# RWKV-7 stage of a hybrid encoder layer on one Trainium2 core: the 16x16 substitution emitted behind the first products of the next unit, without ties to other operations

## Chip, cores and metric

The kernel runs on one core of a Trainium2 chip. Its time is the device time of one execution in microseconds (us), the median of the runs. Five engines work side by side, each through a list of instructions of its own, in order: TensorE (PE in the rows, its weight loads PEld), VectorE (DVE), ScalarE (ACT), GpSimd (POOL) and SyncE (SP), which here only issues DMAs.

## What is computed

One layer of an encoder over a sequence of 1024 positions with 1024 features: a combined projection, four sequence mixers (RWKV-7, mLSTM, RG-LRU, HGRN2), a gated sum of the four, and a convolutional feed-forward block. The change lies in the RWKV-7 mixer alone. Cut to its core:

```python
def _rwkv7_scan(r, logw, a, b, k, v):
    # S_t = S_{t-1} diag(w_t) + (S_{t-1} a_t) b_t^T + v_t k_t^T ;  y_t = S_t r_t
    def step(state, inp):
        r_t, lw_t, a_t, b_t, k_t, v_t = inp
        sa = jnp.einsum("bhvk,bhk->bhv", state, a_t)
        state = (state * jnp.exp(lw_t)[:, :, None, :]
                 + sa[..., None] * b_t[:, :, None, :]
                 + v_t[..., None] * k_t[:, :, None, :])
        return state, jnp.einsum("bhvk,bhk->bhv", state, r_t)
    ...
for d in range(2):      # forward and backward over the sequence, 8 heads of 64
    ...
    yd = _rwkv7_scan(*args)
```

The kernel doesn't step through the positions. It takes chunks of 64 and writes the dependence of the positions of a chunk on one another as a triangular system, whose inverse it builds: blocks of 16 by substitution, then blocks of 32 and 64 from these by products. The state passes from chunk to chunk.

## The kernel before

**Units.** `rwkv` works through 16 units, one for each pair of heads (4) and each stretch of 256 positions (4), both directions at once. A unit goes through these functions:

- `rw_lin` and `rw_dir`: decays and gates. `rw_dir` runs once for each direction: a load of its input (`rw_in`, L862, issued by SP), a scan on VectorE (L868), exponentials on ScalarE (L870, L872), GpSimd's L865 before them, then products on VectorE (L882, L884, L888, L890), with copies and products on GpSimd.
- `rw_first`: TensorE's products for the system (L920), masked by VectorE (L928) into `cb`; then the first half of `rw_solve`.
- `rw_solve`: SP sends `cb` out to DRAM (L985) and loads it back in another layout into `SB` (L989) and `pr` (L990). Here the function yields. Its second half is the **substitution**: a copy on ScalarE (L992) of `pr` into `SB`, then on VectorE a copy (L1000) and three rounds (n = 2, 4, 8) of products (L1010) and reduces (L1013), at the end of which `ST` holds the inverse blocks. SP sends `ST` out to DRAM (L1016, two DMAs, tile dT) and loads it back as `R` (L1019).
- `rw_second`: VectorE transposes `R` (L1035); TensorE multiplies (L1040, L1047, L1060, L1068) with VectorE's work between; the result `TF` is written by VectorE (L1071) and ScalarE (L1074).
- `rw_btm`: further products (L968) for the chain.
- `rw_chain`: the chain over the unit's four chunks. For each chunk: TensorE's L1125, ScalarE's copy s (L1128), TensorE's L1135, ScalarE's copy uv (L1138), TensorE's L1143 and L1151, and ScalarE's copy of the state (L1154, into M at the unit's end). The outputs y (L1106, L1110) are copied by ScalarE (L1113).

**The loop.** Step g of the loop runs three units side by side: the chain of the unit before (`prev`), `rw_second` of the current one (`cur`) and `rw_first` of the next (`fst`, `nxt`). It does so in four stages, st = 0 to 3, advancing the generators a piece at a time. Between these, `pieces()` lays 512-column products of the gate projection on TensorE, so that it has something to do while the other engines work; their weights are split into w_hi and w_lo by ScalarE (L116) and GpSimd (L119).

**What sets the order.** TensorE's order in this loop is the order of the code (`manual_schedule`). On the other engines a scheduler decides, from the order in which instructions are emitted, a raised priority for the chain's operations, and ties: inside `issue_after(x)`, instructions are placed behind the instruction x. The second half of `rw_solve`, substitution and DMAs, is emitted by the last `next(fst, None)` at st = 3, inside two such ties: to `self.act_mo`, the chain's last state copy (L1154), and to `self.dve_tf`, the last of the four TF copies on VectorE (L1071):

```python
if st == 3:
    if g + 2 < n:
        lin = self.rw_lin(*order[g + 2], wp)
    with ExitStack() as q:
        if prev is not None:
            q.enter_context(self.tc.issue_after(self.act_mo.ins))
        if cur is not None:
            q.enter_context(self.tc.issue_after(self.dve_tf.ins))
        next(fst, None)
```

Units are numbered here from 0, by the step in which `rw_second` is run on them; "unit 3" in the rows is the turn of the loop in which the L1040 of unit 3 follows the substitution of unit 3.

Of the kernel before, what the change touches and what calls it, by code (L numbers as in the profile page):

```python
# [23 lines left out]
class K:  # L24
# [996 lines left out]
    def rw_second(self, b, wp):  # L1021

        nc = self.nc
        NB = self.NB
        NC = 2 * NB
        cb = b["cb"]

        fl = lambda x: x.rearrange("p d m t -> p (d m t)")
        rs = lambda q: slice(32 * q, 32 * q + 32)

        blk = lambda q, d, m, sb: cb[rs(q), d, m, 32 * sb:32 * sb + 32]
        R = b["R"]
        RT = self.t(wp, [P, 2, NC, 32], "rw_RT")
        E = self.t(wp, [P, 2, NC, 32], "rw_E")
        nc.vector.transpose(fl(RT), fl(R))  # L1035
        dm = [(d, m) for d in range(2) for m in range(NC)]
        pe = self.ps([P, 2, NC, 32], "ps")
        for d, m in dm:
            for q in range(4):
                nc.tensor.matmul(pe[rs(q), d, m, :], lhsT=blk(q, d, m, q % 2), rhs=(RT, R)[d][rs(q), d, m, :],  # L1040
                                 start=True, stop=True, tile_position=(32 * q, 32 * q))
        nc.vector.tensor_tensor(E, pe, self.rw_lm.unsqueeze(2).to_broadcast([P, 2, NC, 32]), op=MUL)
        yield
        pe = self.ps([P, 2, NC, 32], "ps")
        for d, m in dm:
            for q in range(4):
                nc.tensor.matmul(pe[rs(q), d, m, :], lhsT=E[rs(q), d, m, :], rhs=(R, RT)[d][rs(q), d, m, :],  # L1047
                                 start=True, stop=True, tile_position=(32 * q, 32 * q))
        TT, Tn = R, RT
        for d in range(2):  # L1050
            nc.vector.tensor_tensor(TT[:, d], (R, RT)[d][:, d], pe[:, d], op=ADD)
        nc.vector.transpose(fl(Tn), fl(TT))
        yield

        TF = b["TF"] = self.rw_TFt[b["i"] % 2]
        qq = [(d, 2 * hf + d, 2 * hf + 1 - d) for d in range(2) for hf in range(2)]
        pe = self.ps([P, NC, 32], "ps")
        for m in range(NC):
            for d, q0, q1 in qq:
                nc.tensor.matmul(pe[rs(q1), m, :], lhsT=blk(q0, d, m, q1 % 2), rhs=Tn[rs(q0), d, m, :],  # L1060
                                 start=True, stop=True, tile_position=(32 * q0, 32 * q1))
        E3 = self.t(wp, [P, NC, 32], "rw_E")
        nc.vector.tensor_copy(out=E3, in_=pe)
        yield
        pe = self.ps([P, NC, 32], "ps")
        for m in range(NC):
            for d, q0, q1 in qq:
                nc.tensor.matmul(pe[rs(q0), m, :], lhsT=E3[rs(q1), m, :], rhs=TT[rs(q1), d, m, :],  # L1068
                                 start=True, stop=True, tile_position=(32 * q1, 32 * q0))
        for d, q0, q1 in qq:  # L1070
            self.dve_tf = nc.vector.tensor_copy(out=TF[rs(q0), d, :, 32 * (q1 % 2):32 * (q1 % 2) + 32], in_=pe[rs(q0)])  # L1071
        with self.tc.issue_after(self.act_uv.ins) if self.act_uv is not None else ExitStack():
            for q in range(4):
                nc.scalar.copy(TF[rs(q), :, :, 32 * (q % 2):32 * (q % 2) + 32], TT[rs(q)])  # L1074
        yield

    def rw_chain(self, b, wp):


        nc = self.nc  # L1080
        NB, j = self.NB, b["j"]
        M = self.rw_M
# [3 lines left out]
        NC = 2 * NB  # L1086
# [4 lines left out]
        def both(x, st, h, rows):  # L1091

            v = x[rows, 0, st, h, :]
            w = x[rows, 1, NC - 1 - st, h, :]
            return bass.AP(v.tensor, v.offset, [list(v.ap[0]), [w.offset - v.offset, 2], [1, 64]])
# [22 lines left out]
        for st in range(NC):  # L1118
            cs = (st, NC - 1 - st)
            with prio():  # L1120

                pt = self.ps([P, 2, 64], "pc")
                for d, c in enumerate(cs):
                    for h, hr, _ in halves:
                        nc.tensor.matmul(pt[hr, d, :], lhsT=b["ar"][d][:, c, 0, h, :], rhs=b["mv"][:, d, c, h, :],  # L1125
                                         start=True, stop=True, tile_position=(0, 64 * h))
                s = self.t(wp, [P, 2, 64], "rw_s")
                nc.scalar.copy(s, pt)  # L1128
            yield
            with prio():  # L1130

                pu = self.ps([P, 2, 64], "pc")
                for d, c in enumerate(cs):
                    for h, hr, _ in halves:
                        nc.tensor.matmul(pu[hr, d, :], lhsT=b["TF"][hr, d, c, :], rhs=s[hr, d, :], start=True, stop=True,  # L1135
                                         tile_position=(64 * h, 64 * h))
                for h, hr, _ in halves:
                    self.act_uv = nc.scalar.copy(both(b["uv"], st, h, hr), pu[hr])  # L1138

                pm = self.ps([P, 2, 64], "pc")  # L1140
                for d, c in enumerate(cs):
                    for h, hr, _ in halves:
                        nc.tensor.matmul(pm[hr, d, :], lhsT=b["dg"][hr, d, c, :], rhs=b["mv"][hr, d, c, h, :],  # L1143
                                         start=(d == 0), stop=True, tile_position=(64 * h, 64 * h), skip_group_check=True)
            if st:
                y(st - 1)
            yield
            with prio():
                for d, c in enumerate(cs):
                    for h, hr, _ in halves:  # L1150
                        nc.tensor.matmul(pm[hr, d, :], lhsT=b["btm"][:, d, c, hr], rhs=b["uv"][:, d, c, h, :], start=False,  # L1151
                                         stop=True, tile_position=(0, 64 * h), skip_group_check=True)
                for h, hr, _ in halves:
                    self.act_mo = nc.scalar.copy(M[j][hr, :, h, :] if st == NC - 1 else both(b["mv"], st + 1, h, hr), pm[hr])  # L1154
            if st == NC - 1:
                y(st)
            yield
        for d in range(2):
            n0 = b["n0"][d]
            for h, hr, _ in halves:  # L1160
# [3 lines left out]
                                    in_=src)  # L1164
# [109 lines left out]
    def rwkv(self, dr, dG, es, extra):  # L1274
        nc = self.nc
# [34 lines left out]
        cur = next(gen)  # L1310
# [2 lines left out]
        lin = self.rw_lin(*order[1], wp)  # L1313
        for j in range(self.VA, 4):
            self.rw_v(j, vp)
        prev = None

        with self.tc.manual_schedule(engines={mybir.EngineType.PE}):
            for g in range(n + 1):
                chn = self.rw_chain(prev, wp) if prev is not None else iter(())  # L1320
                sec = self.rw_second(cur, wp) if cur is not None else iter(())
                fst, nxt = iter(()), None
                for st in range(4):

                    next(chn, None)
                    if st > 1:
                        next(sec, None)
                    pieces(1)

                    next(chn, None)  # L1330
                    if st == 0:
                        if cur is not None:
                            self.rw_btm(cur, wp)
                        if g + 1 < n:
                            fst = self.rw_first(*order[g + 1], lin, wp)
                            nxt = next(fst)
                    else:
                        next(fst, None)

                    next(chn, None)  # L1340
                    if st > 1:
                        next(sec, None)
                    if prev is None:
                        pieces(self.GATE0 // 4 - 1)
                    else:
                        credit += rate if g < n else rate + self.ENDF / 2
                        k = int(credit + 1e-6)
                        credit -= k
                        pieces(k)
                    if st == 3:  # L1350
                        if g + 2 < n:
                            lin = self.rw_lin(*order[g + 2], wp)
                        with ExitStack() as q:
                            if prev is not None:
                                q.enter_context(self.tc.issue_after(self.act_mo.ins))
                            if cur is not None:
                                q.enter_context(self.tc.issue_after(self.dve_tf.ins))
                            next(fst, None)
                next(chn, None)
                prev, cur = cur, nxt  # L1360
            for _ in self.filler:
                pass
# [760 lines left out]
```

## Time and profile before

| | us |
|---|---|
| runs | 2766.28, 2766.10, 2759.79 |
| median | 2766.1 |
| profiled execution | 2765.5 |
| its span | 2763.7 |
| TensorE busy (PE) | 2529.6 (92%) |
| its weight loads (PEld) | 2026.5 (73%) |
| VectorE busy (DVE) | 1755.2 (64%) |
| GpSimd busy (POOL) | 1216.7 (44%) |
| ScalarE busy (ACT) | 953.2 (34%) |

The profile is of one execution. The span runs from its first instruction to its last; 1.8 us of the execution lie outside. The shares are means over the whole layer; the loop that the change touches runs from about 420 us to about 1060 us of the span, and what holds it up is to be read there. Idle time counts only on an engine that the end of the span hangs on. Of TensorE's clock the trace says what level was granted, 1.00 for 2.4 GHz and 0.50 for 1.2 GHz; the mean over the span is 0.961.

### The profile page before, as it was taken

How to read it: one execution, taken by the hardware profiler on the slowest of the kernel's cores; microseconds unless marked ns; L12 is line 12 of the kernel's file. 1: busy time of each engine (PE TensorE's matmuls, PEld its weight loads, DVE VectorE, ACT ScalarE, POOL GpSimd, SP SyncE). 2: the span in 40 equal slices, each digit the busy share in tenths (PEclk: the TensorE clock that was granted, in tenths of full speed). 3: DMA queues.
4: the chain of work that ended last, by engine and by line, in shares of the span. 5: the costliest groups of instructions: out<-in, count | busy, mean ns of one | idle time of the engine just before them, and what ended most of it. 6: DMA issues, size and time to landing. Idle time of an engine off the chain costs nothing. (4 is left out here: it accounts for less than half of the span.)

```text
span 2763.7 us, 48164 instructions
## 1 busy us (share of the span) xinstructions
PE 2529.6 (92%) x19138; PEld 2026.5 (73%) x19138; DVE 1755.2 (64%) x2741; ACT 953.2 (34%) x1781; POOL 1216.7 (44%) x1196
## 2 busy tenths in 40 slices
PE   5999888898898899889989989999998999999998
PEld 4777666676676677668777777788776788888887
DVE  6667765665664650665553668357479998896344
ACT  4355533343343342433331332211234344442002
POOL 3654463343443431742222355357555444445332
PEclk9999999999999999999999989999999999999999
DMA  6422243343443433421111444555543222225222
GB/s 211 132 69 65 92 138 91 104 105 97 105 113 83 103 76 113 112 60 43 39 43 29 123 156 153 179 186 164 168 122 96 84 76 88 73 73 196 87 80 77
DMA packets 402395, 290.46 MB, mean 105 GB/s; under 512 B 121339, under 2 KB 364521, under 8 KB 402169
## 3 DMA queue, kind: packets, MB, share of 16 engines
q1 hardware_dynamic: 380600, 252.18, 31.7%
q10 hardware_dynamic: 21568, 35.20, 3.6%
q8 instruction: 150, 2.46, 0.4%
q14 instruction: 77, 0.62, 0.1%
HBM read 223.47 MB, written 63.83 MB: 104 GB/s over the span
## 5 line engine op out<-in xcount | busy, mean ns | idle before, releaser
L119 POOL TENSOR_TENSOR w_lo<-w_raw,w_hi 128x512 fp32r<-128x512 f32 x284 | 393.2, 1385 | 798.3 <-ACT w_hi L116 272.7
L125 PE MATMUL pbig<-uh,w_hi 128*128 128x512 f32 x1208 | 509.7, 423 | 17.7 <-ACT w_hi L116 8.5
L127 PE MATMUL pbig<-uh,w_lo 128*128 128x512 f32 x1208 | 486.2, 404 | 6.1 <-POOL w_lo L119 5.8
L126 PE MATMUL pbig<-ul,w_hi 128*128 128x512 f32 x1184 | 478.3, 404 | 0.0
L125 PEld LDWEIGHTS pbig<-uh,w_hi 128*128 128x128 f32 x1208 | 234.5, 195 | 85.4 <-ACT gt L1239 11.4
L127 PEld LDWEIGHTS pbig<-uh,w_lo 128*128 128x128 f32 x1208 | 234.7, 195 | 62.5 <-POOL w_lo L119 10.2
L126 PEld LDWEIGHTS pbig<-ul,w_hi 128*128 128x128 f32 x1184 | 230.6, 195 | 42.7 <-issue 1.6
L118 DVE CAST w_hi<-w_raw 128x512 fp32r<-128x512 f32 x224 | 136.2, 610 | 174.1 <-PE pbig L126 120.5
L127 PE MATMUL ppc<-uh,w_lo 128*128 128x512 f32 x340 | 133.4, 396 | 1.4 <-POOL w_lo L119 1.0
L125 PE MATMUL ppc<-uh,w_hi 128*128 128x512 f32 x340 | 132.6, 394 | 1.2 <-DVE w_hi L118 1.2
L126 PE MATMUL ppc<-ul,w_hi 128*128 128x512 f32 x320 | 125.4, 392 | 0.0
L125 PE MATMUL ppa<-uh,w_hi 128*128 128x512 f32 x220 | 89.1, 405 | 5.6 <-DVE w_hi L118 5.6
L127 PE MATMUL ppa<-uh,w_lo 128*128 128x512 f32 x220 | 86.9, 395 | 0.8 <-POOL w_lo L119 0.8
L1138 ACT COPY rw_uv<-ppc 64x128 f32<-64x128 f32 x128 | 33.0, 258 | 158.1 <-PE ppc L1135 156.5
L127 PE MATMUL ppy<-uh,w_lo 128*128 128x512 f32 x216 | 85.0, 394 | 1.4 <-POOL w_lo L119 1.0
L1848 ACT CAST w_hi<-s 128x512 fp32r<-128x512 f32 x84 | 52.0, 619 | 97.5 <-PE ppc L126 19.8
L125 PE MATMUL ppy<-uh,w_hi 128*128 128x512 f32 x216 | 85.0, 393 | 0.1
L126 PE MATMUL ppa<-ul,w_hi 128*128 128x512 f32 x208 | 83.5, 402 | 0.0
L126 PE MATMUL ppy<-ul,w_hi 128*128 128x512 f32 x208 | 82.1, 395 | 0.0
L127 PEld LDWEIGHTS ppc<-uh,w_lo 128*128 128x128 f32 x340 | 64.1, 189 | 16.5 <-POOL w_lo L119 1.4
L125 PEld LDWEIGHTS ppc<-uh,w_hi 128*128 128x128 f32 x340 | 64.3, 189 | 15.7 <-DVE w_hi L118 2.1
L204 ACT CAST uh<-h_raw 128x1024 fp32r<-128x1024 f32 x22 | 23.0, 1051 | 148.6 <-PE ppc L127 121.2
(795 smaller groups left out, 6438.8 us busy)
## 6 DMA issues: line engine op xcount, KB each, us to landing
w_raw<-in_w_in_dram SPq DMA_DIRECT2D x172, 256.0 KB
ada_w<-in_ada_w_dram SPq DMA_DIRECT2D x24, 1024.0 KB
s_raw<-in_ffn_up_dram SPq DMA_DIRECT2D x84, 256.0 KB
dG<-gt ACTq DMA_DIRECT2D x64, 256.0 KB
sgt<-dG SPq DMA_DIRECT2D x32, 512.0 KB
rw_in<-dIn SPq DMA_DIRECT2D x32, 384.0 KB
w_raw<-in_ffn_down_dram SPq DMA_DIRECT2D x44, 256.0 KB
dF<-cv SPq DMA_DIRECT2D x22, 512.0 KB
```

Source lines behind the costliest of these rows:

```text
L118: nc.vector.tensor_copy(out=hi, in_=raw[:, k0:k0 + m])
L119: nc.gpsimd.tensor_tensor(lo, raw[:, k0:k0 + m], hi.bitcast(F32), op=SUB)
L125: nc.tensor.matmul(pt, lhsT=wh, rhs=uh, start=start, stop=False)
L126: nc.tensor.matmul(pt, lhsT=wh, rhs=ul, start=False, stop=False)
L127: nc.tensor.matmul(pt, lhsT=wl, rhs=uh, start=False, stop=stop)
L204: nc.scalar.copy(hi, src)
L1138: self.act_uv = nc.scalar.copy(both(b["uv"], st, h, hr), pu[hr])
L1848: nc.scalar.copy(hi, x)
```

## The change

The substitution and its DMAs are no longer emitted at the end of step g but in step g + 1, behind the first piece of the chain there (at st = 0: the first L1125 products and the copy s), and outside any tie. `pend` carries the generator over. The attributes `dve_tf` and `act_mo` go, since nothing reads them any more. No instruction is added or taken out.

```diff
--- before.py
+++ after.py
@@ -1068,7 +1068,7 @@
                 nc.tensor.matmul(pe[rs(q0), m, :], lhsT=E3[rs(q1), m, :], rhs=TT[rs(q1), d, m, :],
                                  start=True, stop=True, tile_position=(32 * q1, 32 * q0))
         for d, q0, q1 in qq:
-            self.dve_tf = nc.vector.tensor_copy(out=TF[rs(q0), d, :, 32 * (q1 % 2):32 * (q1 % 2) + 32], in_=pe[rs(q0)])
+            nc.vector.tensor_copy(out=TF[rs(q0), d, :, 32 * (q1 % 2):32 * (q1 % 2) + 32], in_=pe[rs(q0)])
         with self.tc.issue_after(self.act_uv.ins) if self.act_uv is not None else ExitStack():
             for q in range(4):
                 nc.scalar.copy(TF[rs(q), :, :, 32 * (q % 2):32 * (q % 2) + 32], TT[rs(q)])
@@ -1151,7 +1151,7 @@
                         nc.tensor.matmul(pm[hr, d, :], lhsT=b["btm"][:, d, c, hr], rhs=b["uv"][:, d, c, h, :], start=False,
                                          stop=True, tile_position=(0, 64 * h), skip_group_check=True)
                 for h, hr, _ in halves:
-                    self.act_mo = nc.scalar.copy(M[j][hr, :, h, :] if st == NC - 1 else both(b["mv"], st + 1, h, hr), pm[hr])
+                    nc.scalar.copy(M[j][hr, :, h, :] if st == NC - 1 else both(b["mv"], st + 1, h, hr), pm[hr])
             if st == NC - 1:
                 y(st)
             yield
@@ -1313,7 +1313,7 @@
         lin = self.rw_lin(*order[1], wp)
         for j in range(self.VA, 4):
             self.rw_v(j, vp)
-        prev = None
+        prev, pend = None, iter(())
 
         with self.tc.manual_schedule(engines={mybir.EngineType.PE}):
             for g in range(n + 1):
@@ -1323,6 +1323,8 @@
                 for st in range(4):
 
                     next(chn, None)
+                    if st == 0:
+                        next(pend, None)
                     if st > 1:
                         next(sec, None)
                     pieces(1)
@@ -1350,12 +1352,7 @@
                     if st == 3:
                         if g + 2 < n:
                             lin = self.rw_lin(*order[g + 2], wp)
-                        with ExitStack() as q:
-                            if prev is not None:
-                                q.enter_context(self.tc.issue_after(self.act_mo.ins))
-                            if cur is not None:
-                                q.enter_context(self.tc.issue_after(self.dve_tf.ins))
-                            next(fst, None)
+                        pend = fst
                 next(chn, None)
                 prev, cur = cur, nxt
             for _ in self.filler:
```

On TensorE all stands as before. On three other engines the order is another. The names end in numbers of the program's buffers, which can differ between the two kernels where the same tile is meant.

**ScalarE, at the start of the substitution of unit 3.** Before:

```order
L1138 COPY rw_uv_3406<-ppc_4331 64x2x64 x2
L1074 COPY rw_TF_190_720<-rw_R_3921 32x8x32 x4
L939 COPY rw_tmp_4355<-ppa_4352 2x256
L939 COPY rw_tmp_4358<-ppa_4352 2x256
L1154 COPY rw_M_719_3927<-ppc_4338 64x2x64 x2
L992 COPY rw_SB_4241<-rw_pr_4242 32x256
L1113 COPY rw_ysb_3929<-ppy_4343 128x2x2x64
```

After:

```order
L1138 COPY rw_uv_3406<-ppc_4331 64x2x64 x2
L1074 COPY rw_TF_190_720<-rw_R_3939 32x8x32 x4
L992 COPY rw_SB_4241<-rw_pr_4242 32x256
L939 COPY rw_tmp_4355<-ppa_4352 2x256
L939 COPY rw_tmp_4358<-ppa_4352 2x256
L1154 COPY rw_M_717_3896<-ppc_4338 64x2x64 x2
L1113 COPY rw_ysb_3898<-ppy_4343 128x2x2x64
```

The substitution's first copy, L992, stood behind L939 and the chain's L1154 and stands right behind the TF copies L1074. On VectorE the first ten instructions after it (L1000, four L1010, an L1013, four L1010) move likewise from behind the four L1071 to ahead of them.

**VectorE, in the middle of the substitution of unit 3**, where `rw_dir` of the unit after the next lies between its rounds. Before:

```order
L1013 TENSOR_REDUCE rw_ST_713<-rw_pr_4242 64x2x4x4
L1010 TENSOR_TENSOR rw_pr_4242<-rw_SB_4241,rw_ST_713 64x256
L1013 TENSOR_REDUCE rw_G_4443<-rw_pr_4242 64x32
L868 SCALAR_TENSOR_TENSOR rw_tmp_4549<-rwrs_717,rw_l_788_4429 128x256
L888 SCALAR_TENSOR_TENSOR rw_tmp_4562<-rw_l_789_4431,rw_in_4546 128x256
L1010 TENSOR_TENSOR rw_pr_4242<-rw_SB_4241,rw_ST_713 64x256
L868 SCALAR_TENSOR_TENSOR rw_tmp_4574<-rwrs_717,rw_l_791_4438 128x256
```

After:

```order
L1013 TENSOR_REDUCE rw_ST_713<-rw_pr_4242 64x2x4x4
L1010 TENSOR_TENSOR rw_pr_4242<-rw_SB_4241,rw_ST_713 64x256
L1013 TENSOR_REDUCE rw_G_4461<-rw_pr_4242 64x32
L1010 TENSOR_TENSOR rw_pr_4242<-rw_SB_4241,rw_ST_713 64x256
L1013 TENSOR_REDUCE rw_G_4461<-rw_pr_4242 64x32
L1010 TENSOR_TENSOR rw_pr_4242<-rw_ST_713,rw_G_4461 64x256
L868 SCALAR_TENSOR_TENSOR rw_tmp_4549<-rwrs_717,rw_l_788_4429 128x256
L888 SCALAR_TENSOR_TENSOR rw_tmp_4562<-rw_l_789_4431,rw_in_4546 128x256
L1013 TENSOR_REDUCE rw_ST_713<-rw_pr_4242 64x4x8
```

The first scan of `rw_dir` (L868) stood behind the first reduce into G of the last round (n = 8) and now stands behind that round up to its first L1010 of `ST` and G.

**VectorE, at the end of the substitution of unit 3.** Before:

```order
L890 SCALAR_TENSOR_TENSOR rw_BK_4554<-rw_tmp_4562,rw_tmp_4549 64x4x64 x2
L1013 TENSOR_REDUCE rw_ST_713<-rw_pr_4242 64x4x8
L888 SCALAR_TENSOR_TENSOR rw_tmp_4587<-rw_l_792_4440,rw_in_4571 128x256
L1010 TENSOR_TENSOR rw_pr_4242<-rw_ST_713,rw_G_4443 64x256
L890 SCALAR_TENSOR_TENSOR rw_BK_4579<-rw_tmp_4587,rw_tmp_4574 64x4x64 x2
L1013 TENSOR_REDUCE rw_ST_713<-rw_pr_4242 64x4x8
L1035 STREAM_TRANSPOSE rw_RT_4699<-rw_R_4471 128x256
```

After:

```order
L884 TENSOR_TENSOR rw_AR_4578<-rw_in_4571,rw_l_791_4438 64x4x64
L1013 TENSOR_REDUCE rw_ST_713<-rw_pr_4242 64x4x8
L890 SCALAR_TENSOR_TENSOR rw_BK_4554<-rw_tmp_4562,rw_tmp_4549 64x4x64 x2
L888 SCALAR_TENSOR_TENSOR rw_tmp_4587<-rw_l_792_4440,rw_in_4571 128x256
L890 SCALAR_TENSOR_TENSOR rw_BK_4579<-rw_tmp_4587,rw_tmp_4574 64x4x64 x2
L1035 STREAM_TRANSPOSE rw_RT_4699<-rw_R_4489 128x256
```

The last reduce of the substitution, L1013, stood behind both pairs of L890 and the L888 between and now stands ahead of them. In units of even number an L888 and one pair of L890 change sides in the same way.

**SP, the DMAs that follow, unit 3.** Before:

```order
L838 DMA rw_lw_4977<-dLw_701 128x1024
L862 DMA rw_in_5099<-dIn_699 128x3x256
L1016 DMA dT_703<-rw_ST_713 32x16x16 x2
L1019 DMA rw_R_4471<-dT_703 128x8x32
L862 DMA rw_in_5124<-dIn_699 128x3x256
```

After:

```order
L838 DMA rw_lw_4977<-dLw_701 128x1024
L1016 DMA dT_703<-rw_ST_713 32x16x16 x2
L862 DMA rw_in_5099<-dIn_699 128x3x256
L1019 DMA rw_R_4489<-dT_703 128x8x32
L862 DMA rw_in_5124<-dIn_699 128x3x256
```

One load of `rw_in` (L862) moves from ahead of the two L1016 to between them and the load of `R` (L1019). In units of even number it is the other way round: there one L862 stood between L1016 and L1019, and L1019 now comes right behind L1016.

## Rows read from the trace of the kernel before

**Rows 1.** Waits of TensorE, 380 to 1060 us: total, times, longest.

```profile
PE pps L1040 <- DVE rw_RT L1035: 69.8, 15, 9.9
```

**Rows 2.** Timeline, VectorE, unit 3: start, us, instruction, count [idle before <- releaser].

```profile
518.55 1.24 DVE L1071 COPY rw_TF<-pps 32x128 f32<-32x128 f32 x4 [5.01 <-PE pps L1068]
...
525.09 0.67 DVE L868 TENSOR_TENSOR_SCAN rw_tmp<-rwrs,rw_l 128x256 f32<-128x256 bf16 x1
...
533.50 0.87 DVE L890 SCALAR_TENSOR_TENSOR rw_BK<-rw_tmp,rw_tmp 64x256 f32<-64x256 f32 x2
...
534.73 0.41 DVE L888 SCALAR_TENSOR_TENSOR rw_tmp<-rw_l,rw_in 128x256 f32<-128x256 f32 x1
...
536.66 0.41 DVE L1013 TENSOR_REDUCE rw_ST<-rw_pr 64x32 f32<-64x256 f32 x1
...
542.27 0.45 DVE L1035 STREAM_TRANSPOSE rw_RT<-rw_R 128x256 f32<-128x256 f32 x1 [5.21 <-DMA rw_R<-dT]
```

**Rows 3.** Timeline, ScalarE, unit 3.

```profile
515.76 1.64 ACT L1074 COPY rw_TF<-rw_R 32x256 f32<-32x256 f32 x4
...
518.51 0.64 ACT L992 COPY rw_SB<-rw_pr 32x256 f32<-32x256 f32 x1
...
525.79 0.42 ACT L870 ACTIVATE rw_l<-rw_tmp 128x256 f32<-128x256 f32 x1 [1.64 <-DVE rw_tmp L868]
...
526.12 0.53 ACT L1138 COPY rw_uv<-ppc 64x128 f32<-64x128 f32 x2
```

**Rows 4.** Timeline, TensorE, unit 3.

```profile
526.79 0.45 PE L1151 MATMUL ppc<-rw_uv,rw_btm 128*64 128x64 f32 x8
...
542.77 0.65 PE L1040 MATMUL pps<-rw_RT,rw_cb 32*32 32x32 f32 x32 [3.43 <-DVE rw_RT L1035]
```

**Rows 5.** Timeline, VectorE, unit 4.

```profile
560.41 1.24 DVE L1071 COPY rw_TF<-pps 32x128 f32<-32x128 f32 x4 [5.00 <-PE pps L1068]
...
576.77 0.94 DVE L890 SCALAR_TENSOR_TENSOR rw_BK<-rw_tmp,rw_tmp 64x256 f32<-64x256 f32 x2
...
578.86 0.41 DVE L1013 TENSOR_REDUCE rw_ST<-rw_pr 64x32 f32<-64x256 f32 x1
```

**Rows 6.** Timeline, ScalarE, SP's queue and TensorE, unit 4.

```profile
560.90 0.63 ACT L992 COPY rw_SB<-rw_pr 32x256 f32<-32x256 f32 x1 [0.56 <-DMA rw_pr<-dA]
...
581.07 0.56 SPq L862 DMA_DIRECT2D rw_in<-dIn  x1
...
585.87 0.65 PE L1040 MATMUL pps<-rw_RT,rw_cb 32*32 32x32 f32 x32 [5.33 <-DVE rw_RT L1035]
```

**Rows 7.** Waits of ScalarE, 470 to 1000 us.

```profile
ACT rw_SB L992 <- DMA rw_pr<-dA: 4.4, 7, 1.5
```

**Rows 8.** Timeline, VectorE, unit 15.

```profile
1021.78 1.24 DVE L1071 COPY rw_TF<-pps 32x128 f32<-32x128 f32 x4 [5.01 <-PE pps L1068]
...
1029.34 0.63 DVE L1010 TENSOR_TENSOR rw_pr<-rw_ST,rw_G 64x256 f32<-64x256 f32 x1
```

**Rows 9.** Busy time: unit 1; after a wait; sum of units 2 to 14.

```profile
core 0: us, PE busy (x) PEld busy (x) DVE busy (x) ACT busy (x) POOL busy (x), PEclk, DMA share, GB/s
460.31:475.63 15.32, 15.28 (x341) 11.12 (x341) 6.77 (x13) 6.44 (x19) 2.71 (x4) 1.00 0.39 106
2109.00:2111.40 2.40, 2.40 (x7) 1.82 (x7) 2.37 (x2) 0.00 (x0) 2.39 (x1) 0.50 0.67 196
...
sum 220.78, PE 220.54 PEld 164.72 DVE 85.44 ACT 76.92 POOL 35.04; mean PE 16.96 PEld 12.67 DVE 6.57 ACT 5.92 POOL 2.70
```

**Rows 10.** Timeline, TensorE, two waits.

```profile
460.31 0.45 PE L1040 MATMUL pps<-rw_RT,rw_cb 32*32 32x32 f32 x32 [1.36 <-DVE rw_RT L1035]
...
2108.62 0.80 PE L127 MATMUL ppc<-t4h,w_lo 128*128 128x512 f32 x1 [2.23 <-DVE w_lo L1850]
```

**Rows 11.** Timeline, VectorE and GpSimd, unit 3.

```profile
521.30 0.44 DVE L1010 TENSOR_TENSOR rw_pr<-rw_SB,rw_ST 64x64 f32<-64x64 f32 x2
...
522.09 1.54 DVE L1010 TENSOR_TENSOR rw_pr<-rw_ST,rw_G 64x64 f32<-64x64 f32 x2
522.16 1.35 POOL L119 TENSOR_TENSOR w_lo<-w_raw,w_hi 128x512 fp32r<-128x512 f32 x1 [2.79 <-ACT w_hi L116]
```

## The prediction, made before the changed kernel ran

> **What bounds the kernel now.** TensorE is busy 92% of the span, so I began with what it waits for. In the RWKV-7 loop nearly all of it is one wait, before the first product of `rw_second` (L1040): 69.8 us in 15 units [rows 1]. Unit 3 shows the way there. VectorE copies TF (L1071), runs the 16x16 substitution mixed with the next unit's `rw_dir`, ends it with the reduce at 536.66, and 5.2 us later (two DMAs, dT out and R back) transposes R at 542.27 [rows 2]. TensorE, idle for 3.43 us by then, starts L1040 at 542.77 [rows 4]. In unit 4 the same wait is 5.33 us [rows 6]. So a substitution that ends earlier lets TensorE start earlier, until TensorE has something else to wait for. Units 2 to 14 (13 of them) run like this, odd ones like unit 3 and even ones like unit 4.
>
> **A second cost hangs on that wait.** From L1040 to L1068 the 13 units take 220.78 us together; unit 1, with the same 341 matmuls, takes 15.32 us at a granted clock of 1.00 [rows 9]. At that pace the 13 would take 199.2, so 21.6 us go to the 1.2 GHz level after the idle time. Unit 1 had waited 1.36 us and kept 2.4 GHz; elsewhere a wait of 2.23 us was followed by a clock of 0.50 [rows 9, 10].
>
> **The change, part by part.** No instruction is added or removed; the substitution is emitted later, and two ties are gone.
>
> *When it starts.* The tie to the TF copies held the substitution behind them; now it is placed ahead of them and starts once ScalarE's copy L992 is done. In unit 3 L992 ran at 518.51, behind the two L939 and the two L1154; it now follows L1074, which ends at 517.40 [rows 3]. If its load has landed it ends at 518.04, if not, at the latest at 519.15 as now. VectorE's block (TF copies, substitution, `rw_dir`), which began at 518.55 [rows 2], thus begins between 0.5 us earlier and 0.6 later; I take 0.05 later, the middle. In unit 4 L992 itself waited for the load, till 560.90 [rows 6], as it did in 7 of the 13 units [rows 7]. It can't move there: it ends at 561.53, and the block, which began at 560.41 [rows 5], begins 1.12 later. The ten small operations that now run ahead of the TF copies therefore gain nothing by themselves; in even units they cost.
>
> *When it ends.* The block holds the same work: 18.52 us in unit 3 (518.55 to 537.07), without gaps. What moves is its inside: the last reduce now stands ahead of a last L890 pair, an L888 and, in odd units, one more L890 pair. That is 0.87 + 0.41 + 0.87 = 2.15 us in odd units [rows 2], 0.41 + 0.94 = 1.35 in even ones [rows 2, 5]. The end of the substitution moves by 0.05 - 2.15 = -2.1 us (odd) and by 1.12 - 1.35 = -0.2 (even).
>
> *The DMAs behind it.* On SP, R's load changes places with `rw_in` loads. From the reduce's end to the transpose it takes 5.20 us in unit 3 [rows 2], and 585.87 - 0.50 - 579.27 = 6.10 in unit 4, where an `rw_in` load was issued at 581.07, between dT and R [rows 5, 6]. The new order puts such a load between in odd units and takes it out in even ones. I count the whole 0.9 us, the difference of the two rows, against odd units and for even ones; the lower bound is 0 in both. The transpose, and with it L1040, moves by -2.1 + 0.9 = -1.2 (odd) and by -0.2 - 0.9 = -1.1 (even).
>
> *What pays for it.* The first scan of `rw_dir` (L868) stands deeper in the block. It began 525.09 - 518.55 = 6.54 us into it [rows 2]. Now it stands behind the substitution up to the first L1010 of ST and G in the last round; in unit 15, where no `rw_dir` is mixed in, that point comes 1029.34 + 0.63 - 1021.78 = 8.19 us into the block [rows 8]. L868 is later by 1.65 us plus the block's own shift: 1.7 in odd units, 2.8 in even ones. ScalarE's L870 waits for it (1.64 us already), and in order behind L870 stands L1138, the chain's uv [rows 3], which TensorE's L1151 needs: uv ends at 526.65, L1151 starts at 526.79 [rows 4]. With 0.14 us of slack, L1151 gets a new wait of about 1.55 us (odd; 1.0 to 2.1) and 2.6 us (even).
>
> *Who is late next.* TensorE reaches L1040 later by that wait: 539.34 + 1.55 = 540.9 in unit 3, and L1040 is released at 542.77 - 1.2 = 541.6, so a wait of 0.7 is left; in unit 4, 580.54 + 2.6 = 583.1 against 585.87 - 1.1 = 584.8, and 1.6 is left. R is still what ends last, so the gain counts: 6 x 1.2 + 7 x 1.1 = 14.9 us. Unit 1 had little to give: its new wait of some 2.3 us meets a stall of 1.36 [rows 10] and costs about 1 us. Together -14 us.
>
> *Work behind the moved copy.* With L992 ahead, ScalarE's L939 and L1154 run later by its length and its wait, up to 0.63 + 0.56 = 1.2 us in unit 4 [rows 6]. L1154 writes the chain's state M, which GpSimd copies for the next chain's first product, L1125; no row names L1125 as waiting. The price is 0 to 1.2 us a unit, and I take 0: two weight pieces on TensorE (12 products) and two L845 groups stand before that L1125. The stores of ysb behind them on SP have no reader in the loop.
>
> *The clock.* If only 0.7 and 1.6 us of waiting are left before L1040, near the 1.36 us that left the clock alone, most of the 21.6 us comes back. But the new waits at L1151, up to 2.6 us, lie on both sides of the 2.23 us that was followed by 0.50; half speed there is partly hidden by the 0.7 and 1.6 us left at L1040. Bounds 0 and 21.6; I take two thirds, 14.4, since the nearer row is unit 1's.
>
> *Sum.* -14 - 14.4 = -28.4 us. The profiled execution took 2765.5 us (span 2763.7), 0.6 below the median, so 2737 by the one and 2737.7 by the other.
>
> *A rule on the block's length.* Beside GpSimd's L119 (522.16, 1.35 us), an L1010 pair took 1.54 us where its twin before it took 0.44 [rows 11]. The Trainium skill's page GPSIMD Engine Reference, section 8 (Key points), says that GpSimd shares its SBUF interfaces with VectorE and contends with VectorE instructions that have two SBUF inputs. By that rule the block isn't a fixed 18.5 us, since the substitution's products will meet other GpSimd work than now; this is the third rival below. The row agrees with it.
>
> **The rivals.**
> 1. *The half speed moves along.* The waits at L1151 lower the clock as often as those at L1040 did. For it: 2.6 us is above 2.23. Against it: the odd units' 1.55 is nearer to 1.36. Then only the 14 us stay: 2752.
> 2. *The new wait takes the place of the old one.* Half speed after L1151 lasts so long that TensorE comes to L1040 some 3.3 us later still (an estimate: behind L1040 half speed costs 21.6 / 13 = 1.7 us a unit, and I double it). It arrives at 544.2 in unit 3 (+1.4) and 586.4 in unit 4 (+0.5), in all 6 x 1.4 + 7 x 0.5 = +12 us and 1 for unit 1, against 21.6 won behind L1040: 2757.
> 3. *Slower: VectorE stretched by GpSimd.* If products of the substitution that now run alone come to lie beside `rw_dir`'s GpSimd work, at the price of [rows 11], 1.1 us each time, the substitution ends later. It decides from 1.2 us a unit on. With two such meetings L1040 moves by -1.15 + 2.2 = +1.05, 13 times, and the clock stays as it is: +14 us, 2780. Against it: GpSimd's list of work is the same, so a product that meets it newly takes the place of another.
> 4. *It does nothing:* the scheduler's new order ends the substitution where it ended, since the later start eats what the tail gives: 2766.
>
> **How the numbers follow.** The measurement can tell about 0.3%, 8.3 us, from no change: 2757.8 and below is faster. Forecast 0.52 (2720 to 2748), rival 1 0.21, rival 2 0.13, rival 3 0.08, rival 4 0.06. The predicted time is 2738. The low end takes the best of the bounds: odd units 0.5 us earlier at the start and no 0.9 on R, (6 x 2.65 + 7 x 1.1) + 21.6 = 45 us, 2721. The high end takes in rivals 1 and 2: 2762, which leaves out rivals 3 and 4. Faster: 0.52 + 0.20 + 0.04 = 0.76; slower 0.08; the rest, 0.16, the same.
>
> **What would show it.** Right: the waits for L1040 fall from 69.8 us to some 25; L1151, with 0.14 us of slack now, waits some 25 to 30 us for uv, which is behind L870 and L868; stretches from L1040 to L1068 are nearer 15.3 than 17.0 us. Wrong: L1040's wait is unchanged (the end of the substitution did not move, or R's load came later than 0.9 us); the granted clock is 0.50 behind L1151 in most units (rival 1 or 2); VectorE's block is longer than 18.9 us (rival 3).

## The result, and the profile after

The changed kernel takes 2735.7 us (median of 4 runs, 2726.0 to 2741.8) against 2765.6 before: a ratio of 0.9893, with a 95% interval of 0.9859 to 0.9928. The profiled execution has a span of 2740.0 us. Forecast were 2738 us and a range of 2721 to 2762.

The waits of TensorE in the loop, 380 to 1060 us (total, times, longest):

```profile
PE pps L1040 <- DVE rw_RT L1035: 28.0, 13, 8.3
PE ppc L1151 <- ACT rw_uv L1138: 18.9, 15, 2.5
```

L1040 waits 28.0 us where it waited 69.8 [rows 1]. 8.3 of it are unit 0, before which the loop has nothing to run, so units 1 to 15 wait 19.7. L1151, which had waited for next to nothing, now waits 18.9. Busy time by stretch (us, then PE, PEld, DVE, ACT, POOL busy, granted clock, DMA share, GB/s) for units 3 and 4, L1040 to L1068, and the sum over units 2 to 14:

```profile
539.48:554.82 15.34, 15.30 (x341) 11.12 (x341) 6.77 (x13) 5.41 (x15) 3.08 (x5) 1.00 0.38 102
581.78:597.98 16.20, 16.20 (x341) 12.31 (x341) 6.87 (x14) 5.17 (x15) 2.69 (x4) 0.89 0.22 54
...
sum 199.68, PE 199.43 PEld 148.83 DVE 89.19 ACT 69.73 POOL 36.96; mean PE 15.34 PEld 11.45 DVE 6.86 ACT 5.36 POOL 2.84
```

199.7 us stand for 220.8 before [rows 9]: the same matmuls, 21.1 us faster, because the clock fell behind L1040 in 3 of the 13 units only (4, 12 and 14), and not in all of them as before.

The loop and what comes after it, before (first fence) and after (second):

```profile
424.23:1052.36 628.13, 564.21 (x8185) 433.79 (x8185) 366.69 (x870) 238.85 (x670) 238.62 (x366) 0.94 0.38 96
1052.36:2763.70 1711.34, 1616.91 (x9426) 1317.34 (x9426) 1099.66 (x1535) 512.14 (x820) 762.29 (x626) 0.97 0.34 105
```

```profile
423.17:1020.81 597.64, 556.08 (x8185) 427.12 (x8185) 362.97 (x870) 237.89 (x670) 235.77 (x366) 0.97 0.40 100
1020.81:2740.00 1719.19, 1621.52 (x9426) 1321.58 (x9426) 1102.29 (x1535) 512.10 (x820) 760.48 (x626) 0.97 0.34 105
```

The loop is 30.5 us shorter. What comes after it is the same program; its 7.9 us more in this profile are within the spread of single executions (in the runs below it took 1707 to 1719 us), and that is why the two spans differ by 23.7 us and the medians by 29.9.

**Where the 30.5 us come from.** I measured each unit from the end of the L1068 before it. The table has the means of the odd units (3 to 13) and the even ones (2 to 14), in us:

| | odd before | odd after | even before | even after |
|---|---|---|---|---|
| end of the substitution | 18.47 | 15.90 | 19.04 | 18.12 |
| from there to the transpose of R | 5.40 | 6.04 | 6.04 | 6.87 |
| TensorE ready for L1040 | 20.77 | 21.80 | 20.30 | 23.24 |
| L1040 begins | 24.38 | 22.45 | 25.58 | 25.49 |
| L1040 to L1068 | 17.28 | 15.35 | 16.73 | 15.37 |

L1040 begins 1.93 us earlier in odd units and 0.09 in even ones: 6 x 1.93 + 7 x 0.09 = 12.2 us. The stretches behind it give 21.1. Unit 1's L1040 begins 2.0 us later, and unit 0's stretch is 0.8 longer. Together 30.5.

An odd unit, number 3, on VectorE, ScalarE and TensorE:

```profile
517.26 0.17 DVE L1000 COPY rw_ST<-rw_SB 64x8 f32<-64x8 f32 x1 [4.82 <-ACT rw_SB L992]
...
518.50 1.23 DVE L1071 COPY rw_TF<-pps 32x128 f32<-32x128 f32 x4
...
524.93 0.67 DVE L868 TENSOR_TENSOR_SCAN rw_tmp<-rwrs,rw_l 128x256 f32<-128x256 bf16 x1
...
532.70 0.41 DVE L1013 TENSOR_REDUCE rw_ST<-rw_pr 64x32 f32<-64x256 f32 x1
533.03 0.86 DVE L890 SCALAR_TENSOR_TENSOR rw_BK<-rw_tmp,rw_tmp 64x256 f32<-64x256 f32 x2
...
534.55 1.04 DVE L890 SCALAR_TENSOR_TENSOR rw_BK<-rw_tmp,rw_tmp 64x256 f32<-64x256 f32 x2
...
538.98 0.45 DVE L1035 STREAM_TRANSPOSE rw_RT<-rw_R 128x256 f32<-128x256 f32 x1 [3.38 <-DMA rw_R<-dT]
516.61 0.62 ACT L992 COPY rw_SB<-rw_pr 32x256 f32<-32x256 f32 x1 [0.31 <-DMA rw_pr<-dA]
...
525.64 0.42 ACT L870 ACTIVATE rw_l<-rw_tmp 128x256 f32<-128x256 f32 x1 [2.59 <-DVE rw_tmp L868]
525.96 0.53 ACT L1138 COPY rw_uv<-ppc 64x128 f32<-64x128 f32 x2
526.26 0.73 PE L1151 MATMUL ppc<-rw_uv,rw_btm 128*64 128x64 f32 x8 [0.50 <-ACT rw_uv L1138]
539.48 0.45 PE L1040 MATMUL pps<-rw_RT,rw_cb 32*32 32x32 f32 x32 [0.58 <-DVE rw_RT L1035]
```

The last reduce ends at 533.11, ahead of all L890 as the order had it. L1040 waits 0.58 us where it waited 3.43 [rows 4], and L1151 waits 0.50 for uv, which stands behind L870 on ScalarE.

An even unit, number 4, with the DMAs (ACTq and SPq are the issues on these queues):

```profile
555.92 0.64 ACT L992 COPY rw_SB<-rw_pr 32x256 f32<-32x256 f32 x1 [2.16 <-DMA rw_pr<-dA]
...
565.09 0.42 ACT L870 ACTIVATE rw_l<-rw_tmp 128x256 f32<-128x256 f32 x1 [4.79 <-DVE rw_tmp L868]
565.71 0.97 PE L1151 MATMUL ppc<-rw_uv,rw_btm 128*64 128x64 f32 x8 [2.50 <-ACT rw_uv L1138]
572.97 0.33 ACTq L1240 DMA_DIRECT2D dG<-gt  x1
573.56 1.31 SPq L1016 DMA_DIRECT2D dT<-rw_ST  x2
573.85 0.33 ACTq L1240 DMA_DIRECT2D dG<-gt  x1
578.95 0.37 SPq L1019 DMA_DIRECT2D rw_R<-dT  x1
581.78 0.45 PE L1040 MATMUL pps<-rw_RT,rw_cb 32*32 32x32 f32 x32 [2.88 <-DVE rw_RT L1035]
```

L992 waits for its load, so the block starts late, L868 with it, and L1151 waits 2.50. R's load goes out 5.39 us after dT, since it waits for dT to land; before the change it was 2.81 in this unit. Two stores of the gate projection (L1240) now start beside dT. Before the change they had started some 5 us ahead of it:

```profile
574.11 0.34 ACTq L1240 DMA_DIRECT2D dG<-gt  x1
574.99 0.33 ACTq L1240 DMA_DIRECT2D dG<-gt  x1
579.30 1.27 SPq L1016 DMA_DIRECT2D dT<-rw_ST  x2
582.11 0.37 SPq L1019 DMA_DIRECT2D rw_R<-dT  x1
```

### The profile page after: what moved, and what is told of

It reads as the page before. It is cut to its first block, busy times and chain, and to the rows that moved or that the text cites. A ratio compares the mean times of both kernels' runs of the same rounds, so it can differ in the third digit from the quotient of the medians.

```text
span 2740.0 us, 48186 instructions
## 1 busy us (share of the span) xinstructions
PE 2527.0 (92%) x19138; PEld 2024.4 (74%) x19138; DVE 1754.6 (64%) x2741; ACT 952.3 (35%) x1781; POOL 1212.6 (44%) x1196
## 5 line engine op out<-in xcount | busy, mean ns | idle before, releaser
L119 POOL TENSOR_TENSOR w_lo<-w_raw,w_hi 128x512 fp32r<-128x512 f32 x284 | 393.4, 1386 | 751.8 <-DVE w_hi L118 266.4
L1909 DVE SCALAR_TENSOR_TENSOR cv<-z,colsB,cv 128x1024 f32<-128x1024 f32 x44 | 59.4, 1351 | 20.2 <-ACT cv L1908 20.2
```

Source lines behind the costliest of these rows:

```text
L119: nc.gpsimd.tensor_tensor(lo, raw[:, k0:k0 + m], hi.bitcast(F32), op=SUB)
L1909: nc.vector.scalar_tensor_tensor(cv, z[:, 1:T + 1], self.c("cw1", ct), cv, op0=MUL, op1=ADD)
```

## The experiments

All ratios are against runs of the kernel before on the same chip.

**1. The ties alone, and the place alone.** First the old place without ties:

```diff
                         if g + 2 < n:
                             lin = self.rw_lin(*order[g + 2], wp)
-                        with ExitStack() as q:
...
-                            next(fst, None)
+                        next(fst, None)
```

> One part of the change alone: the substitution is emitted where it was, at the end of stage 3, without either tie. The scheduler then gives the same order of instructions on every engine as for the changed kernel. Theory (the ties are the whole change, the place does nothing): 2736 us, within 8. Rival (the place matters): nearer to 2765 us.

Then the new place with both ties:

```diff
...
                     next(chn, None)
+                    if st == 0:
+                        with ExitStack() as q:
+                            for x in ties:
+                                if x is not None:
+                                    q.enter_context(self.tc.issue_after(x.ins))
+                            next(pend, None)
...
```

(`ties` holds the last L1154 and the last L1071 of the step before; `pend` carries the generator over as in the changed kernel.)

> The other part alone: the substitution is emitted at the new place, behind the first products of the next unit's chain, with both ties kept. The order on every engine is that of the kernel before. Theory: 2765 us, within 5. Rival (the place matters): nearer to 2736 us.

Without ties 2738.1 us (0.9907, 0.9892 to 0.9922); at the new place with ties 2763.9 (0.9999, 0.9990 to 1.0009). The ties are the whole change. Which of these two places the substitution is emitted at makes no difference that can be measured, with the ties or without them.

**2. Each tie by itself.** The tie to L1154 dropped, that to the TF copies kept:

```diff
-                            if prev is not None:
-                                q.enter_context(self.tc.issue_after(self.act_mo.ins))
```

> Substitution at its old place, with the tie to the TF copies (VectorE's last L1071) kept and the tie to the chain's last state copy (ScalarE's L1154) dropped. ScalarE's order is then that of the changed kernel (L992 right behind L1074), VectorE's order that of the kernel before. Theory (the gain comes from the earlier end of the substitution on VectorE, not from L992): the end of the substitution does not move, L1040 waits some 65 to 70 us as before, L1151 waits for nothing, and the time is that of the kernel before, 2766 us, within 5. Rival (L992's earlier start is what counts): the waits of L1040 fall by a third or more, 2750 us or less.

2765.5 us (1.0006, 0.9992 to 1.0019); L1040 waits 68.7 us. The earlier L992 is worth nothing while the tie to the TF copies stands. And the reverse:

```diff
-                            if cur is not None:
-                                q.enter_context(self.tc.issue_after(self.dve_tf.ins))
```

> The other half: the tie to the chain's last state copy (L1154) kept, the tie to the TF copies dropped. L992 stays behind L1154; on VectorE only L1000 moves ahead of the TF copies; in odd units one pair of L890 (0.87 us) moves behind the last L1013, in even units none does. Theory: odd units gain some 0.9 us each, 6 x 0.9 = 5 us, and the waits left before L1040 (2.5 and 5.4 us) still bring the clock down: 2760 us. Rival (the tie to the TF copies was the whole matter): as the changed kernel, 2736 us.

2751.6 us (0.9958, 0.9942 to 0.9975), a larger gain than the 2760 us expected. What I had missed is SP: in even units R's load also comes ahead of the second `rw_in` load here, and with dT landing as before (2.86 us) the way from the substitution to the transpose falls from 6.04 to 5.24 us there. So 0.8 us is what that load between dT and R costs on the mean of the seven (0.9 in six; in unit 14 no such load stood there before). The 13 stretches took 208.5 us, so a part of the clock came back too. The two ties do not simply add up: one gives 0.0%, the other 0.4%, both together 1.1%.

**3. The clock by itself.** The kernel before, with products that nobody reads on TensorE in its wait before L1040 (`KEEP`: their number in even and in odd units):

```diff
-        nc.vector.transpose(fl(RT), fl(R))
+        with self.tc.high_priority(offset=self.HP): nc.vector.transpose(fl(RT), fl(R))
...
-        pe = self.ps([P, 2, NC, 32], "ps")
+        pe = self.ps([P, 2, NC, 32], "ps"); self.keep(pe, b)
...
+    KEEP = (18, 13)
+
+    def keep(self, pe, b):
+        o = pe.rearrange("p d m t -> p (d m t)")
+        if 2 <= b["i"] <= 14:
+            for i in range(self.KEEP[b["i"] % 2]):
+                self.nc.tensor.matmul(o, lhsT=self.uh[i % 8][:, :P], rhs=self.uh[i % 8][:, :256], start=True, stop=True)
```

> The kernel before, with products that nobody reads (128x128 by 256 columns, into the PSUM tile that L1040 then overwrites) on TensorE in its wait before L1040: 18 of them in even units, 13 in odd ones, units 2 to 14, sized to take some 3.8 us of the 5.4 and 2.7 us of the 3.4. No step of the computation changes. Theory of the clock: what is lost from L1040 to L1068 hangs on TensorE's idle time before L1040; with that filled, the 13 stretches go at 1.00 and take 195 us in place of 220.8: some 20 to 25 us less, 2743 us. Rival (the clock falls there for another reason, or that half speed is hidden by other waits): 2766 us, or more where the added products delay L1040.

2750.1 us (0.9959, 0.9946 to 0.9972). The products took only 2.3 and 1.85 us, so waits of some 3.0 (even) and 1.8 us (odd) were left, and the clock still fell behind 9 of the 13. The raised priority of the transpose moved nothing that shows: from the substitution to it took 5.70 us on the mean, 5.74 before. Hence a second run with `KEEP = (36, 23)` and the transpose as it was:

> The kernel before with more of the products that nobody reads: 36 before L1040 in even units and 23 in odd ones. In the run with 18 and 13 they took 2.3 and 1.85 us, left waits of 2.96 and 1.76 us, and the 13 stretches from L1040 to L1068 fell from 220.8 to 210.2 us. Theory: with waits under 0.8 us left everywhere and L1040 released when it was before, all 13 stretches go at full clock, 195 us: 2763 - 25 = 2738 us. Rival (a part of the half speed there does not hang on the wait): 2750 us as with fewer products, or more.

2737.3 us (0.9909, 0.9891 to 0.9927). The waits of TensorE and the sum of the 13 stretches:

```profile
PE pps L1040 <- DVE rw_RT L1035: 20.1, 15, 9.5
...
sum 195.16, PE 194.89 PEld 145.76 DVE 80.35 ACT 76.86 POOL 35.01; mean PE 14.99 PEld 11.21 DVE 6.18 ACT 5.91 POOL 2.69
```

Not one stretch is slowed any more: 195.2 us for 220.8. L1040 begins when it did before (25.02 us behind the L1068 before it, in both on the mean), so the 25.6 us in these stretches are the clock's. They make up nearly all of the 27 us that this run gains, and that is nearly what the whole change gives, though nothing that L1040 waits for came earlier. (The scheduler also placed some work behind the loop in another order; the loop by itself is 26.1 us shorter.)

**4. Does R still set the pace?** The changed kernel with the transpose of R three times in a row:

```diff
-        nc.vector.transpose(fl(RT), fl(R))
+        for _ in range(3): nc.vector.transpose(fl(RT), fl(R))
```

> The changed kernel, with VectorE's transpose of R (L1035, 0.45 us) done three times in a row, so that L1040 is released 0.9 us later; the result is the same. Theory (R still ends last before L1040 in the changed kernel): 13 x 0.9 = 12 us more, and the clock falls behind the longer waits in the other four even units too, 4 x 1.5 = 6: 2748 to 2756 us. Rival (TensorE is bound by its own work and by L1151 there, R has slack): under 2741 us.

2756.7 us (0.9974, 0.9960 to 0.9988), 21 us more than the changed kernel. L1040 began 1.08 us later in a unit on the mean, 14 us in all, and the 13 stretches took 208.3 us in place of 199.7. R does end last, and a microsecond on its way costs some 1.5 here.

**5. Why dT lands late in even units.** The changed kernel with the gate stores held back:

```diff
+                self.act_s = nc.scalar.copy(s, pt)
...
             for k in range(8):
+                if k == 2:
+                    with self.tc.issue_after(self.act_s.ins) if self.act_s is not None else ExitStack():
+                        for o, x in st:
+                            nc.scalar.dma_start(out=o, in_=x)
+                    st = []
...
-                nc.scalar.dma_start(out=dG[i][:, sl], in_=g)
+                st.append((dG[i][:, sl], g))
...
```

(`act_s` is the chain's last copy s, L1128. What is left in `st` is stored behind the last gate tile.)

> The changed kernel, with the stores of the gates (L1240, two of 256 KB for each gate tile) held back on ScalarE until behind the third piece of the next gate tile and the chain's copy s before it, so that in even units they no longer start beside the DMAs of dT. Theory: dT landed late in even units (4.46 us from its issue to that of R, 2.84 before the change) because these stores shared the DMA engines; now it lands in under 3.2 us there. Rival (rw_in's load, issued 2 us ahead of dT, is the cause): it stays above 4 us. The scheduler also puts uv ahead of L870 in odd units, so the time is not that of the stores alone: 2712 to 2730 us by theory.

2721.4 us (0.9839, 0.9812 to 0.9865). Unit 8 of the changed kernel, then of this one:

```profile
728.05 0.55 SPq L862 DMA_DIRECT2D rw_in<-dIn  x1
730.02 1.30 SPq L1016 DMA_DIRECT2D dT<-rw_ST  x2
734.12 0.37 SPq L1019 DMA_DIRECT2D rw_R<-dT  x1
729.51 0.33 ACTq L1240 DMA_DIRECT2D dG<-gt  x1
730.39 0.33 ACTq L1240 DMA_DIRECT2D dG<-gt  x1
```

```profile
722.40 0.55 SPq L862 DMA_DIRECT2D rw_in<-dIn  x1
724.37 1.27 SPq L1016 DMA_DIRECT2D dT<-rw_ST  x2
727.28 0.37 SPq L1019 DMA_DIRECT2D rw_R<-dT  x1
```

`rw_in` is loaded 2.0 us ahead of dT in both; without the stores beside it R goes out 2.91 us after dT, with them 4.10. Over the even units the mean falls from 4.46 to 3.32, where under 3.2 was expected. That is most of the 1.62 us by which dT had come later, not all: unit 4 stays at 4.36, unit 14 at 3.74. The trace shows what else lay on the way there. The DMA queues of unit 4 from dT's issue to R's (571.53 to 575.89 us; packets, MB, share of 16 engines):

```profile
q1 hardware_dynamic: 1319, 0.32, 31.5%
q8 instruction: 1, 0.02, 1.3%
```

The first row holds the DMAs that SP issued. The second is a transfer of 16 KB that the profile calls `instruction`, which I take for the loading of code. It starts 1.92 us behind dT's issue in unit 4, 0.91 us in unit 14; units 10 and 12 (3.44 and 3.14) have one of 16 or 8 KB too, while in units 2, 6 and 8 (2.81 to 2.91) none starts in the first 2.3 us. In the changed kernel the three latest even units (4, 10 and 14, 4.82 to 5.39) have such transfers among dT's packets, unit 8 (4.10) has one at their end, and units 2, 6 and 12 (3.68 to 4.33) have none; before the change, unit 13 had one and took 3.76. So the stores are the larger cause and these transfers the likely rest; no experiment moved them by themselves. Of the 14 us that this kernel gains on the changed one a part is another order of ScalarE and VectorE in odd units (uv ahead of L870).

**6. The new wait at L1151.** The changed kernel with `rw_dir`'s exponentials tied behind uv:

```diff
-        G = sw
-        nc.scalar.activation(G, cum, AF.Exp, scale=-CW)
-        iG = cum
-        nc.scalar.activation(iG, cum, AF.Exp, scale=CW)
+        G, iG = sw, cum
+        with self.tc.issue_after(self.act_uv.ins) if self.act_uv is not None else ExitStack():
+            nc.scalar.activation(G, cum, AF.Exp, scale=-CW)
+            nc.scalar.activation(iG, cum, AF.Exp, scale=CW)
```

> The changed kernel, with ScalarE's exponentials of rw_dir (L870, L872) tied behind the chain's uv copies (L1138). uv no longer waits for the scan L868. The scheduler also draws the last reduce of the substitution ahead of four more VectorE products (L882, L884, some 3 us). Theory (R's way sets the pace, and TensorE's wait at L1151 costs only where R does not end later): both waits go, L1151's 18.9 us to about 0 and L1040's 19.7 us (units 1 to 14) to under 8; the time falls by 20 to 35 us against the changed kernel, to 2700 to 2716 us. Rival (another input is late next: L920, which waits for the L890 that now stand behind): the two waits turn into one at L920, and the time stays at 2736 us within 8.

2704.8 us (0.9788, 0.9767 to 0.9808), 31 us faster than the changed kernel and the fastest of all here. Its waits:

```profile
PE ppc L1125 <- ACT rw_mv L1154: 13.3, 11, 2.0
PE pps L1040 <- DVE rw_RT L1035: 12.6, 7, 9.5
```

L1151 waits for next to nothing (0.2 us), L1040 for 3.1 us outside unit 0, and the loop has 7 us at the granted clock of 0.50 where the changed kernel had 40. The tie did two things, though: the substitution also ends 3.4 us earlier on the mean. A new wait is there, smaller: the chain's state copy stands behind the exponentials on ScalarE. So I tied these behind L1154 instead, and emitted `rw_dir` behind the third piece of the chain:

```diff
...
                             self.rw_btm(cur, wp)
-                        if g + 1 < n:
-                            fst = self.rw_first(*order[g + 1], lin, wp)
-                            nxt = next(fst)
                     else:
                         next(fst, None)
...
                     next(chn, None)
+                    if st == 0 and g + 1 < n:
+                        fst = self.rw_first(*order[g + 1], lin, wp)
+                        nxt = next(fst)
```

> As e3_uv, but rw_dir is emitted behind the third piece of the chain and its exponentials are tied behind the chain's first state copy (L1154), so that neither uv nor this copy waits for the scan. In e3_uv the wait had moved to L1125 (13.3 us), which needs that copy. Theory: the wait at L1125 goes and R or L920 takes over a part: 2692 to 2702 us, against 2704.8. Rival (R was as late as TensorE in e3_uv, so L1040 waits instead): no change, 2702 to 2708 us.

2733.3 us (0.9890, 0.9861 to 0.9919): neither theory came true. Its waits:

```profile
PE ppa L920 <- DVE rw_BK L890: 19.7, 7, 3.6
PE ppt L920 <- DVE rw_BK L890: 14.9, 7, 5.1
```

From unit 1 on L1040 no longer waits for R, nor the chain for its copies; L920 waits 34.6 us for L890, and the loop has 62 us at the granted clock of 0.50. VectorE's block carries two things that TensorE needs, the substitution for L1040 and `rw_dir` for L920. Here the substitution stands ahead of the first L882, and what it gained L890 lost. The later place of `rw_dir` and the other tie went in together, so their shares are not told apart.

## Why the prediction held, step by step

**What bounds the kernel: right.** R was the last thing that L1040 waited for, and in the changed kernel it still is in 12 of the 13 units (experiment 4).

**When the substitution ends: right.** Forecast were -2.1 us (odd) and -0.2 (even); -2.6 and -0.9 came. In unit 3 the block began 0.2 us earlier, since L992's load had landed soon after L1074, and what now stands behind the last reduce takes 2.48 us (533.11 to 535.59), not 2.15. In even units the block began 0.95 us later on the mean, near the 1.12 forecast, but was itself 0.4 us shorter.

**The DMAs behind it: wrong in even units.** I took 0.9 us off there, since no `rw_in` load stands between dT and R any more. That gain is real (experiment 2), but dT lands 1.62 us later, for the most part since the gate's stores now start beside it (experiment 5). The step looked at SP's queue alone and not at what ScalarE's queue would send at that time. So even units gained 0.09 us at L1040 instead of 1.1. Odd units gained 1.93 instead of 1.2: the substitution ended earlier, and with the load between dT and R the way grew by 0.6 us, not 0.9.

**What pays for it: right in kind.** L1151 waits for uv, uv for L870, L870 for L868, as forecast. The size was 18.9 us, not 25 to 30: even units waited 1.9 us on the mean (1.1 to 2.5) for the 2.6 forecast, odd ones 0.7 for 1.55. L868 stands less deep in the block than I had taken from unit 15: in unit 3 it begins 7.67 us into it, not 8.19 [rows 8].

**The clock: right, and too small.** 14.4 us of the 21.6 were to come back behind L1040; 21.1 did. The reason that I gave holds for odd units only: 0.7 us of waiting was left there as forecast, but in even ones 2.25 in place of 1.6, as long as the 2.23 us that was followed by a clock of 0.50 [rows 9, 10], and still the clock stayed in four of the seven. At full clock the 13 stretches take 195.2 us, not 199.2, because even units are faster than unit 1, an odd one, by which I had priced them all. So 25.6 us had been lost there.

**The sum.** -28.4 was forecast, -29.9 measured. The order gave less than expected (12.2 us less 2.0 in unit 1, against 14.9 less 1) and the clock more. Within the order, odd units gave 11.6 us for 7.2 and even ones 0.6 for 7.7. The errors have opposite signs, so that the total is within 2 us is luck.

**The rivals.** The half speed did move along in part (the first rival). Behind the 2.50 us wait of unit 4's L1151 the granted clock was 0.50:

```profile
566.00:569.30 3.30, 3.30 (x13) 2.66 (x13) 3.19 (x7) 2.65 (x7) 3.16 (x7) 0.50 0.75 167
```

It fell behind that wait in seven turns of the loop (units 1, 2, 4, 8, 10, 13 and 14). Experiment 6 took these waits away, but moved the end of the substitution too, so it doesn't price them alone. The second rival did not come: in even units TensorE was ready for L1040 2.94 us later, 1.0 more than its new waits, and R still ended behind it. VectorE was not stretched (the third): in unit 3 its block, with the L890 at its end, runs from 517.26 to 535.59, 18.3 us for 18.5. Products still meet GpSimd, but others than before: the L1010 at 521.55 beside L119 takes 1.27 us, the next of its shape 0.61, and the pair that took 1.54 [rows 11] takes 0.44:

```profile
520.76 0.44 DVE L1010 TENSOR_TENSOR rw_pr<-rw_ST,rw_G 64x64 f32<-64x64 f32 x2
521.05 1.29 POOL L119 TENSOR_TENSOR w_lo<-w_raw,w_hi 128x512 fp32r<-128x512 f32 x1 [2.77 <-ACT w_hi L116]
...
521.55 1.27 DVE L1010 TENSOR_TENSOR rw_pr<-rw_SB,rw_ST 64x256 f32<-64x256 f32 x1
...
523.30 0.61 DVE L1010 TENSOR_TENSOR rw_pr<-rw_SB,rw_ST 64x256 f32<-64x256 f32 x1
```

The rule cited from the Trainium skill (GPSIMD Engine Reference, section 8) agrees with these rows, and the sum did not change by it.

**What is not settled.** How long a wait must be for the clock to fall. In the changed kernel it fell behind waits of 2.34, 2.66 and 2.88 us at L1040 and not behind 2.17 and 2.18. Without ties at the old place a wait of 2.61 left it alone, and in the first run of experiment 3 it fell behind 1.76 in one unit and not behind 3.07 and 3.10 in two others. The length alone doesn't decide it.

## What to carry to other kernels

A tie that holds work behind an instruction on one engine also fixes what can be mixed with that work on the others; try it without, several ties together too, and read the order that results. Price a wait of TensorE at more than its length: here the half clock behind it cost 25.6 us beside 59.9 us of waiting (outside unit 0), and products that nobody reads won that back alone. When a step moves in time, look at every queue that will send at its new time, not only at the queue it stands in.

## What the runs showed that I had not expected

With a pair of 256 KB stores on another queue beside it, a small write to DRAM (dT, two DMAs of 32 KB) takes longer: R's load, which waits for it, goes out 4.46 us after the write was issued in place of 2.84 (mean of seven units), and 3.32 us after it with the stores held back. The Trainium skill's page DMA: Bandwidth & Descriptors, section "Latency and other measured facts", gives the latency of an HBM access as 0.2 us on average and 2 us at high load. No run here tells such a latency apart from packets that take turns.

And 18 products of 128x128 by 256 columns took 2.3 us, 0.13 us each, where I had counted 0.21.
